# Rotation tables and memory's rstd made without matmuls, in a one-layer decoder kernel

## The chip, the cores and the metric

The kernel runs on one core of one Trainium2 chip. The metric is the device time of one execution in microseconds, as the median of the runs. The engines are named as in the profile: PE is TensorE's matmul side and PEld its weight loads, DVE is VectorE, ACT is ScalarE, POOL is GpSimd, SP is SyncE, which here only issues DMAs. A "q" after a name (SPq) means the engine's sequencer, which issues and waits.

## The reference

One decoder layer on 256 tokens of 1024 features, all in float32. `B` is 1.

```python
h = x + W_out( sig(g_a) * (MoBA(n1 x) W_br_a) + sig(g_b) * (HGRN2(n1 x) W_br_b) )
h = h + CrossAttn(n2 h, n_mem mem)        # 4 heads of 256; mem is 256 tokens
h = h + SwiGLU(n3 h)                      # hidden width 2816
out = rmsnorm(h, final_norm_g)

def rmsnorm(x, g): return x * rsqrt(mean(x * x, -1) + EPS) * g

def rope(t, pos):                          # on q and k of MoBA, 16 heads of 64
    ang = pos[:, None, :, None] * inv_freq # inv_freq = 10000 ** (-arange(0, 64, 2) / 64)
    t1, t2 = t[..., :32], t[..., 32:]
    return concatenate([t1 * cos(ang) - t2 * sin(ang), t2 * cos(ang) + t1 * sin(ang)], -1)
```

Two parts of it matter here: the cosines and sines of `rope` for 256 positions and 32 frequencies, and the rstd of the memory tokens (`rsqrt` of the mean square), which scales the values and the scores of the cross-attention.

## The kernel before

Every weight matrix is read from HBM in chunks of 1 MB (128 partitions x 2048). `prep` loads one chunk (`raw`, L255 to L261), ACT makes its rounded copy `hi` (L266), and DVE makes the rest `lo = raw - hi` (L270). Three matmuls (hi x hi, hi x lo, lo x hi) then give products of full precision. There are three buffers each for `raw`, `hi` and `lo`, and `nxt` prepares chunks two ahead (LEAD = 2). A `raw` buffer comes free when DVE has made `lo`, so SP's next load waits for that.

The order of PE's instructions is the order of the program. The order on ACT, DVE and SP is made by a planner that takes the instruction of the highest rank (the earliest in the program) that it expects to be ready; POOL's order is the program's until L869 or so. Each engine then executes its own list in order, and an instruction that has to wait holds those behind it. On SP this concerns loads: a DMA that waits for data holds the weight loads behind it.

Background work runs in generators. `tick()` is called after each half or whole unit of a matrix product and moves every generator on to its next `yield`. So a `yield` puts what follows one unit (some 5.5 us of PE) later in the program.

The stages in the order of time: the forget gate's matrix with x's norm (to 28 us); the q of HGRN2 (`psf`, to 51); values (`pst`, to 98); q and k of MoBA with rotation (`ev_rope`, to 145); gates and both attentions (to 260); output projections (to 307); the cross-attention, where chunks of q and k alternate with the products P1 to P7 of a Strassen-like scheme for v (to 383); SwiGLU (to 576); the final norm and the stores.

The pieces that the change touches:

- Constants: `cst` (128 x 512 float32) holds the identity for transposes and the causal mask; `lm` (128 x 144) holds HGRN2's masks; `gv` holds gains, the 32 frequencies in each partition and two positions per partition.
- x's rstd: `H` holds the tokens in rows (`xtok`, 1 MB, one transfer, L576). ACT squares both halves with a running sum (L624), `rstd_of` makes `r_x` on POOL (L385), and `rows_of` (L391 to L393) spreads it over partitions by two transposes on PE and a copy on ACT. `spread` places these transposes in the middle of the product for head 5.
- Tables: `rope_tables` reduces the angles on POOL with tokens in partitions, takes both Sin on ACT (L503, L504), and multiplies by `r_x` into `CS` (L507). `angles` (L756) transposes `CS` by four transposes on PE, and ACT copies the result to `turnsF`, with frequencies in partitions and tokens in columns.
- Memory: `mraw` holds memory with features in partitions. `memory()` scales and splits it, squares it in place on ACT (L398), adds pieces on DVE (L401 to L405), and four small matmuls with `ones` sum over partitions (`ssq`, L410). `rows_of` spreads the result by two transposes and a copy. The rows are used in `scores`, the rstd itself in `ev_vx`.
- The last loads: `fetch` (L1431) splits the last loads of SwiGLU into two transfers each.
- The tail: for the second token half, POOL multiplies columns 0 to 512 and 512 to 640 by the final gain, DVE columns 640 to 1024 (L1695); ACT and DVE then scale by the rstd and the stores go out.

Of the kernel before, what the change touches and what calls it, by code (L numbers as in the profile page):

```python
# [12 lines left out]
F32 = mybir.dt.float32  # L13
# [29 lines left out]
C_W = 544  # L43
# [107 lines left out]
def constants():  # L151
# [7 lines left out]
    c[:, C_IF:C_IF + 32] = (10000.0 ** e.astype(np.float64)).astype(np.float32)  # L159
# [14 lines left out]
def build(tc, A, out):  # L174
    nc = tc.nc
    V, SC, G, PE, SY = nc.vector, nc.scalar, nc.gpsimd, nc.tensor, nc.sync
    with ExitStack() as ctx:
# [32 lines left out]
        cst = cp.tile([128, C_IF], F32, name="cst")  # L210
        gv = cp.tile([128, 90], F32, name="gv")
        lm = cp.tile([128, 144], I32, name="lm")
        ifq, posi = gv[:, 56:88], gv[:, 88:90].bitcast(I32)
        nhalf = cp.tile([128, 4], F32, name="nhalf")
        ident = cst[:, C_ID:C_ID + 128]
# [180 lines left out]
        def square(raw, c):  # L396
            a = slice(2 * c, 2 * c + 2)
            SC.activation(raw[:, a], raw[:, a], AF.Square)  # L398
            if c % 2 == 1:
                b = slice(2 * c - 2, 2 * c)  # L400
                V.tensor_tensor(raw[:, a], raw[:, a], raw[:, b], op=ALU.add)  # L401

        def feature_sum(raw):
            V.tensor_tensor(raw[:, 2:4], raw[:, 2:4], raw[:, 6:8], op=ALU.add)
            V.tensor_tensor(raw[:, 2], raw[:, 2], raw[:, 3], op=ALU.add)  # L405

        def feature_rstd(raw, name):
            ps = bank("ssq", (128, 2))
            for t in range(2):
                PE.matmul(ps[:, t:t + 1], raw[:, 2, t * 128:(t + 1) * 128], ones, start=True, stop=True)  # L410
            return rstd_of(ps, name)

# [41 lines left out]
        tables = big("B12", "tables", (128, 1024))  # L454
        CS = tables[:, 0:512].rearrange("p (c i n f) -> p c i n f", c=2, i=2, n=4)
        turnsF = tables[:, 512:1024].rearrange("p (c t) -> p c t", c=2)

        def rope_tables():
            posf = small("posf", [2])
            G.tensor_copy(posf, posi)  # L460
            q = cp.tile([128, 7, 2, 32], F32, name="rt")
# [41 lines left out]
            tc.keep_in_program_order(SC.activation(m, r, AF.Sin))  # L503
            tc.keep_in_program_order(SC.activation(mh, t, AF.Sin))  # L504
# [70 lines left out]
        SY.dma_start(cst, A["cst"])  # L575
        SY.dma_start(H, A["xtok"])  # L576
# [175 lines left out]
        def angles():  # L752
            b = bank("cs", (128, 2, 2, 128))
            for c in range(2):
                for i in range(2):
                    PE.transpose(b[:, c, i], CS[:, c, i].rearrange("p n f -> p (n f)"), ident)  # L756
            SC.activation(turnsF, b.rearrange("p c i t -> p c (i t)"), AF.Copy)

        def hgrn():
# [11 lines left out]
            angles()  # L771
# [169 lines left out]
        def quad(j):  # L941
# [8 lines left out]
            for ss in sc:  # L950
                mx, nm, sums = small("amx", [4]), small("anm", [4]), small("asum", [4])
                two = [t2("ap", (128, 384)) for _ in range(2)]
                for e, (ps, p) in enumerate(zip(ss, two)):
                    for i, (u, w) in enumerate(parts):
                        z = 2 * e + i
                        V.tensor_tensor_reduce(out=p[:, u:w], in0=ps[:, u:w], in1=cst[:, C_MA + u:C_MA + w],
# [125 lines left out]
        def memory():  # L1082
# [15 lines left out]
            mem["rows"] = rows_of(mem["r"], "m", "rowsB")  # L1098
# [680 lines left out]
```

## Time and profile before

| | |
|---|---|
| runs | 588.11, 588.11, 588.49 us, median 588.11 |
| profiled execution, its own time | 588.42 us |
| span of the profiled execution | 586.5 us, 9105 instructions |
| busy in the span | PE 99%, PEld 83%, DVE 78%, ACT 67%, POOL 24% |
| DMA | 155.63 MB, mean 265 GB/s |

The span is the time from the first to the last instruction of the trace; the execution's own time has 1.9 us more around it. Busy time of PE is the union of its matmuls, whose ends are modelled. The trace's views used below are: the busy line, the waits by engine, the chain of waits that ended last (each step followed back to what released it), the timeline of an engine, a tile's instructions, and the DMA issues.

### The profile page before, as it was taken

Reading aid. Unit: us, or ns where it says so; the run is one execution under the profiler, and the core shown is the slowest. Engines: PE = TensorE matmul, PEld = TensorE weight load, DVE = VectorE, ACT = ScalarE, POOL = GpSimd, SP = SyncE. Lnnn points to the kernel's source line nnn. Section 1 sums busy time; section 2 is a strip of 40 time slices with the busy share of each in tenths; the row PEclk is TensorE's granted clock in tenths of the full one; section 3 lists DMA queues with packets and bytes.
Section 4 is the critical chain, followed back from the end, with each engine's and each line's share of the span. In section 5 each row is a group of like instructions: output and inputs, shape, how many; then the busy total and the mean of one; then the engine's idle time right before and its main releaser. Section 6 shows DMA issues by size and latency. Waiting matters only on the chain.

```text
span 586.5 us, 9105 instructions
## 1 busy us (share of the span) xinstructions
PE 579.4 (99%) x3491; PEld 488.5 (83%) x3491; DVE 459.0 (78%) x650; ACT 392.2 (67%) x646; POOL 139.3 (24%) x141
## 2 busy tenths in 40 slices
PE   9999999999999999999999999999999999999995
PEld 7888888888888888888888889988888888888884
DVE  6789968899868774858868786887878788787944
ACT  6796565564686576657459576777858586776744
POOL 4589500466203600003202333200001010100004
PEclk9999999999999999999999999999999999999998
DMA  8865997496993899599866895976879979995801
GB/s 333 339 217 225 326 382 278 153 312 264 268 378 99 225 308 281 202 379 254 253 242 192 277 374 216 244 268 256 353 294 268 391 175 385 259 392 170 310 1 72
DMA packets 22778, 155.63 MB, mean 265 GB/s; under 512 B 2816, under 2 KB 3840, under 8 KB 6528
## 3 DMA queue, kind: packets, MB, share of 16 engines
q1 hardware_dynamic: 18416, 129.12, 56.1%
q0 software_dynamic: 3456, 25.17, 21.9%
q10 hardware_dynamic: 864, 0.77, 0.4%
q8 instruction: 27, 0.44, 0.3%
q14 instruction: 15, 0.12, 0.1%
HBM read 154.00 MB, written 28.31 MB: 311 GB/s over the span
## 4 chain that ended last, share of the span: by engine, by line
PE 94%; DMA 3%; POOL 1%; SPq 0%; ACT 0%; DVE 0%; issue 0%; POOLq 0%; DVEq 0%; ACTq 0%
PE psf L348 13%; PE pqA L1176 11%; PE pst L323 10%; PE pst L325 10%; PE pst L324 10%; PE psf L350 7%; PE pqF L1176 6%; PE acc L323 3%; PE acc L324 3%; PE acc L325 3%; PE pqB L1176 3%; DMA H<-xtok 2%; PE pso L325 1%; PE pso L324 1%; PE pso L323 1%; PE as L946 1%
## 5 line engine op out<-in xcount | busy, mean ns | idle before, releaser
L270 DVE TENSOR_TENSOR lo<-raw,hi 128x1024 fp32r<-128x1024 f32 (+1 forms) x126 | 159.1, 1283 | 33.8 <-ACT hi L266 33.4
L266 ACT ACTIVATE hi<-raw 128x1024 fp32r<-128x1024 f32 (+1 forms) x126 | 125.9, 1028 | 36.1 <-PE pst L325 20.0
L323 PE MATMUL pst<-hi,XX 128*128 128x512 f32 x160 | 63.6, 397 | 0.0
L325 PE MATMUL pst<-hi,XX 128*128 128x512 f32 x160 | 62.4, 390 | 0.0
L324 PE MATMUL pst<-lo,XX 128*128 128x512 f32 x160 | 62.3, 390 | 0.0
L1422 DVE TENSOR_TENSOR lo<-raw,hi 128x2048 fp32r<-128x2048 f32 (+1 forms) x21 | 41.6, 1983 | 11.4 <-ACT hi L1414 11.4
L348 PE MATMUL psf<-XX,hi 128*128 128x512 f32 x192 | 46.7, 392 | 0.0
L1414 ACT ACTIVATE hi<-raw 128x1024 fp32r<-128x1024 f32 x36 | 36.3, 1052 | 13.9 <-PE acc L325 10.3
L348 PEld LDWEIGHTS psf<-XX,hi 128*128 128x128 f32 x192 | 35.1, 188 | 6.8
L323 PEld LDWEIGHTS pst<-hi,XX 128*128 128x128 f32 x160 | 30.0, 188 | 6.9 <-issue 0.7
L325 PEld LDWEIGHTS pst<-hi,XX 128*128 128x128 f32 x160 | 30.0, 188 | 6.4
L336 ACT ACTIVATE ku<-psf 128x256 f32<-128x256 f32 x40 | 15.1, 380 | 30.3 <-PE psf L348 21.5
L324 PEld LDWEIGHTS pst<-lo,XX 128*128 128x128 f32 x160 | 30.1, 188 | 5.9
L1422 DVE TENSOR_TENSOR lo<-b,hi 128x2048 fp32r<-128x2048 f32 x12 | 27.5, 2288 | 9.3 <-ACT hi L1414 9.2
L1414 ACT ACTIVATE hi<-b 128x1024 fp32r<-128x1024 f32 x24 | 24.2, 1053 | 10.4 <-DMA b<-w 5.5
L323 PE MATMUL acc<-hi,hids 128*128 128x512 f32 x70 | 27.4, 392 | 0.0
L325 PE MATMUL acc<-hi,hids 128*128 128x512 f32 x70 | 27.3, 389 | 0.0
L324 PE MATMUL acc<-lo,hids 128*128 128x512 f32 x70 | 27.2, 389 | 0.0
L350 PEld LDWEIGHTS psf<-XX,lo 128*128 128x128 f32 x192 | 24.6, 191 | 0.9
L350 PE MATMUL psf<-XX,lo 128*128 128x256 f32 x192 | 24.9, 283 | 0.0
L1176 PE MATMUL pqA<-hi,SS 128*128 128x512 f32 x72 | 23.9, 393 | 0.0
L1462 POOL DMA_DIRECT2D b<-w x3 | 2.6, 882 | 82.5 <-DVE fu L1528 51.0
(457 smaller groups left out, 1464.7 us busy)
## 6 DMA issues: line engine op xcount, KB each, us to landing
raw<-w SPq DMA_DIRECT2D x72, 1024.0 KB, 6.6
t<-w POOLq DMA_DIRECT2D x13, 1024.0 KB, 12.2
b<-w SPq DMA_DIRECT2D x10, 1024.0 KB, 8.0
raw<-t SPq DMA_DIRECT2D x10, 1024.0 KB, 9.0
b<-w POOLq DMA_DIRECT2D x7, 1024.0 KB, 8.2
raw<-w SPq DMA_DIRECT2D x10, 512.0 KB, 6.9
rawx<-w SPq DMA_DIRECT2D x4, 1024.0 KB, 8.8
b<-t POOLq DMA_DIRECT2D x4, 1024.0 KB, 12.6
```

The lines of the kernel that those rows point to most:

```text
L266: SC.activation(hi[:, a], raw[:, a], AF.Copy)
L270: V.tensor_tensor(lo[:, a], raw[:, a], hi[:, a].bitcast(F32), op=ALU.subtract)
L323: PE.matmul(ps, xh, h, start=first, stop=False)
L324: PE.matmul(ps, xh, l, start=False, stop=False)
L325: PE.matmul(ps, xl, h, start=False, stop=last)
L336: SC.activation(u, ps[:, 1], AF.Copy)
L348: PE.matmul(ps, w[0][:, k, a], X2[:, k], start=begin, stop=end, skip_group_check=m == 1)
L350: PE.matmul(ps[:, 0], w[1][:, k, a], X2[:, k, 0], start=begin, stop=end, skip_group_check=m == 1)
L946: PE.matmul(ps[:, o], qT[r, j, w, q], kT[r, j, w, 0:q.stop], start=w == 0, stop=w == 1)
L1176: PE.matmul(ps, x[k], z[:, k], start=first and k == 0 and i == 0, stop=k == 3 and i == 2, skip_group_check=not first)
L1414: pin(SC.activation(hi[:, a], raw[:, a], AF.Copy))
L1422: pin(V.tensor_tensor(lo[:, a], raw[:, a], hi[:, a].bitcast(F32), op=ALU.subtract))
```

## The change

- The identity becomes a tile of its own (`ident`, 64 KB); the causal mask moves to `lm`, which grows from 72 to 264 KB and is loaded after `H`, as before.
- `H` is loaded in two transfers, one for each half of the tokens.
- The sixth chunk behind the first is prepared in the loop of `last_half`, at m = 2, instead of by the next `nxt`.
- The tables' angles are made with frequencies in partitions (four groups of 32) and 64 positions in columns. After the Sin, SP writes both waves to a DRAM tile, reads them back spread over partitions into `turnsF`, and POOL multiplies by x's rstd in rows. `angles` goes.
- Memory is loaded a second time with tokens in rows (`mtok`, 1 MB, into the buffer of `mraw`). ACT squares it with a running sum; `rstd_of` makes the rstd. SP writes it to a DRAM tile and reads it back as a row in all partitions, behind P2's load. Squares, additions, `ssq` and memory's `rows_of` go.
- Seven instead of five of the last units of SwiGLU are loaded in two transfers each.
- In the tail DVE multiplies columns 512 to 1024 by the gain, and POOL's piece of 128 columns goes.

```diff
-        cst = cp.tile([128, C_IF], F32, name="cst")
-        lm = cp.tile([128, 144], I32, name="lm")
+        ident = cp.tile([128, 128], F32, name="ident")
+        lm = cp.tile([128, 528], I32, name="lm")
+        tri = lm[:, 144:528].bitcast(F32)
...
+        turnsF = big("B12", "turnsF", (128, 2, 256))
+        waves = dr.tile([32, 2, 256], F32, name="waves")
...
-            for i in range(2):
-                G.tensor_scalar(ang[:, i], ifq, posf[:, i:i + 1], None, op0=ALU.mult)
+            G.tensor_copy(ang, posi)
+            G.tensor_scalar(ang, ang, ifq, None, op0=ALU.mult)
...
-            for i in range(2):
-                for c, z in enumerate((mh, m)):
-                    G.tensor_scalar(CS[:, c, i], bc(z[:, i], 4, 1), r_x[:, i:i + 1], None, op0=ALU.mult)
+            yield 1
+            SY.dma_start(waves.rearrange("f c (g t) -> g f c t", g=4), q[:, 1:3])
+            yield 1
+            yield 1
+            SY.dma_start(turnsF, waves.rearrange("(o f) c t -> o f c t", o=1).to_broadcast([4, 32, 2, 256]))
+            yield 1
+            yield 1
+            for c in range(2):
+                G.tensor_tensor(turnsF[:, c], turnsF[:, c], rows_x, op=ALU.mult)
...
-        SY.dma_start(cst, A["cst"])
-        SY.dma_start(H, A["xtok"])
+        SY.dma_start(ident, A["ident"])
+        for t in range(2):
+            SY.dma_start(H[:, t], A["xtok"][:, t])
...
             last_half(1, m, w, spread if m == 1 else None)
+            if m == 2:
+                run(prep())
...
-            angles()
...
-                if k % 2 == 1:
-                    square(raw, k // 2)
...
-            feature_sum(raw)
             yield 1
-            mem["r"] = feature_rstd(raw, "m")
+            mtok = big("B11", "mtok", (128, 2, 1024))
+            SY.dma_start(mtok, A["mtok"])
             yield 1
+            ssqm = small("ssqm", [2])
+            for t in range(2):
+                SC.activation(mtok[:, t], mtok[:, t], AF.Square, accum_out=ssqm[:, t:t + 1])
+            mem["r"] = rstd_of(ssqm, "m")
             yield 1
-            mem["rows"] = rows_of(mem["r"], "m", "rowsB")
+            mem["neg"] = cp.tile([128, 2], F32, name="r_neg")
+            V.tensor_scalar(mem["neg"], mem["r"], -1.0, None, op0=ALU.mult)
+            rd = dr.tile([2, 128], F32, name="rd")
+            SY.dma_start(rd.rearrange("t p -> p t"), mem["r"])
+            for _ in range(6):
+                yield 1
+            mem["rows"] = cp.tile([128, 256], F32, name="rows_m", tag="rowsB")
+            with tc.issue_after(loaded["P2"]):
+                SY.dma_start(mem["rows"], rd.rearrange("(o t) p -> o (t p)", o=1).to_broadcast([128, 256]))
...
-            n = 2 if made_u[0] > len(units) - 5 else 1
+            n = 2 if made_u[0] > len(units) - 7 else 1
...
-            gain(G, hg1[:, 512:640], 1, 512, 640)
-            gain(V, hg1[:, 640:1024], 1, 640, 1024)
+            gain(V, hg1[:, 512:1024], 1, 512, 1024)
```

## Rows read from the trace of the kernel before

**Rows 1.** The page's busy line: busy us (share of the span) x instructions.

```profile
PE 579.4 (99%) x3491; PEld 488.5 (83%) x3491; DVE 459.0 (78%) x650; ACT 392.2 (67%) x646; POOL 139.3 (24%) x141
```

**Rows 2.** Waits of PE: line, waited for, total us, times, longest us.

```profile
PE warm L423 <- PEq L1770: 0.8, 1, 0.8
PE rb L391 <- POOL r_x L385: 0.2, 1, 0.2
PE psg L598 <- ACT hi L266: 0.2, 1, 0.2
```

**Rows 3.** Chain of waits, 0 to 80 us: start us, us, what.

```profile
8.84 12.29 DMA H<-xtok
...
21.21 2.20 ACT junk L624 x4
...
24.47 0.43 PE rb L391 x2
...
26.75 0.95 PE psg L589 x8
```

**Rows 4.** Timeline of PE: start us, us, engine, line, operation, out<-in, forms, count.

```profile
23.12 1.11 PE L589 MATMUL psg<-XX,lo 128*128 128x256 f32 x8
...
81.25 0.66 PE L756 MATMUL cs<-cst,tables 128*128 128x128 f32 x4
81.66 0.48 PE L323 MATMUL pst<-hi,XX 128*128 128x512 f32 x1
...
313.19 0.38 PE L391 MATMUL rb<-cst,r_m 128*128 128x128 f32 x2
313.40 1.04 PE L1136 MATMUL h1T<-cst,H 128*128 128x128 f32 x8
```

**Rows 5.** Chain of waits, whole span.

```profile
301.03 0.34 PE ssq L410 x4
```

**Rows 6.** Timeline of SP, first 20 us.

```profile
8.84 0.45 SPq L576 DMA_DIRECT2D H<-xtok  x1
```

**Rows 7.** The page's DMA issues: out<-in, count, KB each, median us to landing.

```profile
raw<-w SPq DMA_DIRECT2D x72, 1024.0 KB, 6.6
...
raw<-w SPq DMA_DIRECT2D x10, 512.0 KB, 6.9
```

**Rows 8.** Timelines of ACT, SP and DVE, 56 to 76 us.

```profile
56.37 0.24 ACT L504 ACTIVATE rt<-rt 128x64 f32<-128x64 f32 x1
...
60.89 6.99 SPq L257 DMA_DIRECT2D raw<-w  x3
...
72.85 2.01 ACT L266 ACTIVATE hi<-raw 128x1024 fp32r<-128x1024 f32 x2 [1.68 <-DMA raw<-w]
...
73.94 2.36 DVE L270 TENSOR_TENSOR lo<-raw,hi 128x1024 fp32r<-128x1024 f32 x2 [1.27 <-ACT hi L266]
```

**Rows 9.** Tiles mraw and r_m: count, ns min/median/max, first and last start.

```profile
L1087 ACT ACTIVATE mg<-mraw,gv x8: 495/498/500, 261.8 to 270.0; 128x256 f32<-128x256 f32 x8
...
L1222 ACT ACTIVATE vxh<-fc,r_m x2: 724/726/728, 326.1 to 347.7; 128x512 fp32r<-128x512 f32 x2
```

**Rows 10.** DMA issues from 56 to 84 us, columns as in the page's.

```profile
raw<-w SPq DMA_DIRECT2D x6, 1024.0 KB, 10.0
t<-w POOLq DMA_DIRECT2D x2, 1024.0 KB, 13.9
```

**Rows 11.** Timelines of POOL and DVE in the tail.

```profile
580.34 1.99 POOL L1695 TENSOR_TENSOR hg<-H,gf 128x512 f32<-128x512 f32 x2
...
581.19 0.83 DVE L1695 TENSOR_TENSOR hg<-H,gf 128x384 f32<-128x384 f32 x1
...
582.37 0.68 DVE L1733 TENSOR_SCALAR H<-hg,r_f 128x256 f32<-128x256 f32 x2 [0.22 <-POOL hg L1695]
```

**Rows 12.** Timelines of DVE and PE around P4.

```profile
338.91 2.36 DVE L270 TENSOR_TENSOR lo<-b,hi 128x1024 fp32r<-128x1024 f32 x2 [1.43 <-ACT hi L266]
...
341.87 0.39 PE L1176 MATMUL pqF<-hi,M 128*128 128x512 f32 x1
```

More of the change, by code (lines that the diff above doesn't have):

```diff
@@ L42 @@
 C_ID, C_MA, C_IF = 0, 128, 512
-C_W = 544
+C_W = 513
 V_MIX, V_X, V_MEM, V_FFN, V_HG, V_L0, V_L1 = (8 * i for i in range(7))
@@ L158, in constants @@
     e = -np.arange(0, HD, 2, dtype=np.float32) / np.float32(HD)
-    c[:, C_IF:C_IF + 32] = (10000.0 ** e.astype(np.float64)).astype(np.float32)
+    c[:, C_IF] = np.tile((10000.0 ** e.astype(np.float64)).astype(np.float32), 4)
     m = np.zeros((128, 7, 16), np.int32)
@@ L208, in bank @@
             return sm.tile(list(shape), F32, name=name, tag="sm")
[L210 to L213 removed]
+        ident = cp.tile([128, 128], F32, name="ident")
+        gv = cp.tile([128, 121], F32, name="gv")
+        lm = cp.tile([128, 528], I32, name="lm")
+        tri = lm[:, 144:528].bitcast(F32)
+        ifq, posi = gv[:, 56:57], gv[:, 57:121].bitcast(I32)
         nhalf = cp.tile([128, 4], F32, name="nhalf")
[L215 removed]
         H = big("B0", "H", (128, 2, 1024))
@@ L394, in rows_of @@
             return o
[L396 to L411, printed above, removed]
         XX = big("P2", "XX", (128, 8, 2, 256), F32R)
@@ L451, in build @@
             part_x(k)
-        tables = big("B12", "tables", (128, 1024))
-        CS = tables[:, 0:512].rearrange("p (c i n f) -> p c i n f", c=2, i=2, n=4)
-        turnsF = tables[:, 512:1024].rearrange("p (c t) -> p c t", c=2)
+        turnsF = big("B12", "turnsF", (128, 2, 256))
+        waves = dr.tile([32, 2, 256], F32, name="waves")
         def rope_tables():
-            posf = small("posf", [2])
-            G.tensor_copy(posf, posi)
-            q = cp.tile([128, 7, 2, 32], F32, name="rt")
+            q = cp.tile([128, 7, 64], F32, name="rt")
             ang, m, mh, ml, r, t, u = (q[:, i] for i in range(7))
-            for i in range(2):
-                G.tensor_scalar(ang[:, i], ifq, posf[:, i:i + 1], None, op0=ALU.mult)
+            G.tensor_copy(ang, posi)
+            G.tensor_scalar(ang, ang, ifq, None, op0=ALU.mult)
             def rnd(o, src, c):
@@ L502, in rope_tables @@
                 yield 1
-            tc.keep_in_program_order(SC.activation(m, r, AF.Sin))
-            tc.keep_in_program_order(SC.activation(mh, t, AF.Sin))
-            for i in range(2):
-                for c, z in enumerate((mh, m)):
-                    G.tensor_scalar(CS[:, c, i], bc(z[:, i], 4, 1), r_x[:, i:i + 1], None, op0=ALU.mult)
+            tc.keep_in_program_order(SC.activation(mh, r, AF.Sin))
+            tc.keep_in_program_order(SC.activation(m, t, AF.Sin))
+            yield 1
[7 more added lines that the diff above has]
+                G.tensor_tensor(turnsF[:, c], turnsF[:, c], rows_x, op=ALU.mult)
         rt = rope_tables()
@@ L750, in level @@
                     SC.activation(AT[:, 16 + 4 * g:20 + 4 * g], ps, AF.Copy)
[L752 to L757, printed above, removed]
         def hgrn():
@@ L955, in quad @@
                         z = 2 * e + i
-                        V.tensor_tensor_reduce(out=p[:, u:w], in0=ps[:, u:w], in1=cst[:, C_MA + u:C_MA + w],
+                        V.tensor_tensor_reduce(out=p[:, u:w], in0=ps[:, u:w], in1=tri[:, u:w],
                                                op0=ALU.add, op1=ALU.max, scale=1.0, scalar=-3e38,
@@ L1755 @@
     lg = a["hgrn_lb_logits"]
-    positions = np.ascontiguousarray(a["positions"][0].reshape(2, 128).T).astype(np.int32, copy=False)
+    positions = np.repeat(a["positions"][0].astype(np.int32, copy=False).reshape(4, 64), 32, axis=0)
     arrays = {
@@ L1762 @@
         "mT": feats(a["mem"]),
+        "mtok": tokens(a["mem"]),
         "gv": np.ascontiguousarray(np.concatenate(
@@ L1766 @@
         "gfin": np.ascontiguousarray(a["final_norm_g"].reshape(1, D)),
-        "cst": np.ascontiguousarray(cst[:, :C_IF]),
-        "lm": lm,
+        "ident": np.ascontiguousarray(cst[:, :C_MA]),
+        "lm": np.ascontiguousarray(np.concatenate([lm, cst[:, C_MA:C_IF].view(np.int32)], axis=1)),
     }
```

2 lines of the change are left out of this document (removed).

## Prediction

> **What bounds the kernel now.** I read the page's busy line first: PE is busy for 579.4 us of a span of 586.5, 99% [rows 1]. DVE (78%) and ACT (67%) are loaded but not full, so the question for each edit is only whether it takes time off PE's own sequence, or makes PE wait. The view of PE's waits says where it waits at all: three times, 0.8 us at the very start, 0.2 us for the first converted weights, and 0.2 us at L391, where the transposes that spread x's rstd wait for POOL's `r_x` [rows 2]. Everything between the first 25 us and the end is PE doing matmuls back to back, so matmuls that go are worth their full place in the sequence.
>
> The chain of waits then shows what stands behind the L391 stop: tokens in rows `H<-xtok` are asked for at 8.84 and land 12.29 later, ACT squares both halves from 21.21 for 2.20, POOL makes `r_x`, and the transposes start at 24.47 [rows 3]. The group of eight short matmuls before them began at 23.12 [rows 4], and the next such group takes 0.95 in the chain [rows 3]. PE was therefore free at 23.12 + 0.95 = 24.07, and the hole is 24.47 - 24.07 = 0.40 us. The waits view counts half of it because it lets the pipelined tail of the last matmul count as work.
>
> **The change part by part.**
>
> *Matmuls that go.* The four transposes of the tables (`cs`) begin at 81.25 and the next matmul at 81.66: 0.41 us [rows 4]. The four `ssq` matmuls that sum memory's squares hold the chain for 0.34 us [rows 5]. Memory's two `rb` transposes begin at 313.19 and the next group at 313.40: 0.21 us [rows 4]. PE has no idle time around any of them, so the sum is 0.41 + 0.34 + 0.21 = 0.96 us, all on the path.
>
> *Tokens in rows in two transfers, with a smaller constant ahead of them.* 192 KB (the masks) move from ahead of `H` to behind it, and `H` becomes two transfers of 512 KB. The last square then covers one half, 2.20 / 2 = 1.10 us, instead of two. Counted back from before, the start of the second square stood 24.47 - 21.21 - 1.10 = 2.16 us ahead of the transposes. If the second half lands no later than the whole did (8.84 + 12.29 = 21.13), the transposes are ready at about 21.2 + 2.16 = 23.4, 0.7 us before PE wants them at 24.07. So the hole closes even if the second half lands 0.7 us late. One more issue on SP costs about 0.45 [rows 6] against 192 KB less ahead of it, so I take the whole 0.40 us. The bounds are 0 (the order on ACT eats it) and 0.40 (PE can't start before it is free). The load behind it, the fifth chunk's, is asked for one issue later, into a queue that is busy for longer than that anyway.
> On the size of transfers a row and a page differ. The page of the profile has 512 KB loads landing after 6.9 us and 1024 KB loads after 6.6 [rows 7], so halves are not slower as such. The Trainium skill, "DMA: Bandwidth & Descriptors", section "Rules for kernel authors", asks for at least 1 MiB in one DMA for full bandwidth, which speaks against cutting `H`. By the row the hole closes with 0.7 us to spare; by the page the second half could land later and the sum would be 0.40 us smaller.
>
> *Sixth chunk asked for sooner.* Its load is only ranked ahead of the head-pair work, not made possible sooner, since its buffers come free when earlier chunks are used. It reorders ACT and DVE within the first 60 us; I cost it at 0.
>
> *Tables by transposed angles.* POOL works on 128x64 as before. Its four products with r_x go, and two of twice the size come later. ACT loses a copy. What is added: after the Sin at 56.37 [rows 8], SP writes the waves to memory (pieces of 256 B), waits for them to land, and reads them back. Read and product must be done before the first rotation, some 45 us later, which hides them. What isn't plainly hidden is SP: while it waits to issue the read, the weight loads queued behind it wait too. That is a rival below; in the sum it is 0.
>
> *Memory's rstd from rows.* A load of 1 MB (`mtok`) starts when the last scaling of `mraw` is done, at about 270 [rows 9], and lands by about 280 even at the 10.0 us that loads took in the fullest stretch [rows 10]. Two squares, `r`, and the write of 256 numbers follow. The first user of `r` runs at 326.1 [rows 9], so there are some 40 us of cover. ACT trades four squares for two double ones; DVE loses four additions; both are cheaper or equal. The write of 4-byte pieces has no like in the trace: between 0 and the 13.9 us of the slowest transfers shown [rows 10] it stays covered, so 0. The read of the rows is put on SP behind P2's load, which keeps that load out of its wait.
>
> *The tail.* DVE's last scaling starts at 582.37 because POOL's two gains run from 580.34 for 1.99, to 582.33 [rows 11]. POOL's second gain goes; DVE's becomes 512 columns instead of 384. The 384 took 0.83 from 581.19, with POOL beside them, and the reciprocal follows it. Scaled by columns the 512 take 1.1 and end 0.28 later, which would cancel the gain; but POOL stops early now, so part of that is faster. Bounds 0 and 0.18 (582.37 back to 582.19, if the reciprocal doesn't move); I take 0.10. Two more of the last loads in halves cost two issues on an idle SP: 0.
>
> *Sum.* 0.96 + 0.40 + 0.10 = 1.46 us, bounds 0.96 and 1.54. The profiled execution took 588.42 (span 586.5 and 1.9 around it), which would become 586.96. It is 0.31 above the median of the runs, 588.11, and inside their spread. From the median: 588.11 - 1.46 = **586.65**.
>
> **The rivals.**
>
> *Given back to ACT or DVE (about 587.6).* PE comes sooner to every later stage, by up to 1.36 us at 341.87 (0.40 + 0.96). There P4's first matmul starts; the first half of its low part is ready at 338.91 + 2.36 / 2 = 340.09, which is 1.78 us ahead [rows 12]. If the splits don't move along, 0.4 us are left; one more operation of 1.2 us put ahead of such a split makes PE wait 0.8. For it: the planner orders ACT and DVE anew after such edits. Against it: the splits there are released by PE's own progress, mostly, and move with it, and both engines have less to do. Price 0.5 to 1.4: 587.1 to 588.1.
>
> *The hole stays (587.05).* The new order of loads doesn't bring `r_x` sooner: 588.11 - 0.96 - 0.10. Then the change doesn't do what it says in this part.
>
> *SP stands still on the waves (slower, about 590.8).* The read can be issued only when the write has landed, and SP issues in order. The next three loads were issued from 60.89 on, into a stretch in which DMA is so full that ACT waits until the first of them lands, at 72.85 [rows 8]. The first half of its low part takes half of 2.36 from 73.94, so it is ready at 75.1 [rows 8]. PE wants it at 81.66 [rows 4], in the new kernel 0.40 + 0.41 sooner, at 80.85: 5.7 us to spare. So the wait costs nothing until SP is held past 60.89 + 5.7 = 66.6, and makes the kernel slower by over 0.2% past 66.6 + 1.46 + 1.18 = 69.2. If the waves' write, issued at about 56.9, takes as long as POOL's transfers in this stretch, 13.9 us [rows 10], SP is held to 70.8, PE waits 4.2, and the time is 588.11 - 1.46 + 4.2 = 590.8. Against it: SP's own loads in this stretch took 10.0 at the median [rows 10], which ends at 66.9, about where it starts to cost.
> The Trainium skill, the same page, section "Two DMAs through the same engine are not ordered", has the issuing engine wait for the first transfer's semaphore; so SP's stop is the rule, not a mishap, and only its length is open. No run here shows it yet.
>
> **How the numbers follow.** Forecast, everything hidden: 54%, its own range 586.3 to 587.0. Given back: 21%. Hole stays: 10%. SP held: 15%. A measurement of this kernel can tell about 0.2% (1.2 us) from no change, so faster means below 586.93. The forecast is faster by 0.25%, close to that bound: of its 54% I count 52 as faster, with 3 from the near ends of the two middle cases. The rest of those, 30%, is no change; slower is 15%. The range that leaves out the SP case and little else is 586.1 to 588.4.
>
> **What would show it.** Right: no `cs`, `ssq` or memory `rb` on PE, and the L391 wait gone from PE's waits; `h1T` starts some 1.2 us sooner; the last scaling on DVE waits for no POOL. Wrong: a new line in PE's waits. If it is released by a split of chunks 12 to 14 (75 to 95 us), SP's queue was held; if it lies between 28 and 62 or 313 and 345, the order on ACT and DVE gave the gain back. If `H`'s second half lands after 21.8, the hole stays.

## The result: slower by 0.9%, and the profile after

The changed kernel took 594.05 us (median; 591.08 to 596.3), the kernel before 588.11 beside it: a ratio of 1.0092, 95% interval 1.0071 to 1.0113. The forecast was 586.65. The profiled execution of the changed kernel is the longest of its runs, 596.3 us with a span of 594.5; in the shortest the mean granted clock was 0.999, in this one 0.991, and that difference is part of the story.

Busy line of the page of after, columns as in [rows 1]:

```profile
PE 582.0 (98%) x3481; PEld 488.4 (82%) x3481; DVE 457.6 (77%) x646; ACT 391.2 (66%) x644; POOL 130.7 (22%) x137
```

Every engine but PE has less to do than in [rows 1], and ten matmuls are gone. PE is busy for longer all the same, because some of its matmuls ran slowly. So the time did not come from work. Waits of PE in after, columns as in [rows 2]:

```profile
PE pst L323 <- ACT mm L376: 3.6, 1, 3.6
PE pst L323 <- DVE qu L337: 1.6, 1, 1.6
PE warm L406 <- PEq L1759: 0.8, 1, 0.8
PE psg L585 <- ACT hi L266: 0.3, 1, 0.3
PE psf L348 <- DVE qu L337: 0.2, 1, 0.2
PE pst L325 <- DVE mm L376: 0.2, 1, 0.2
```

The wait for `r_x` at L391 of [rows 2] is gone, as forecast. Two large waits stand in its place. The timeline of PE says where, columns as in [rows 4]:

```profile
23.88 0.38 PE L391 MATMUL rb<-ident,r_x 128*128 128x128 f32 x2
...
52.39 0.47 PE L323 MATMUL pst<-hi,XX 128*128 128x512 f32 x1 [1.63 <-DVE qu L337]
...
83.13 0.50 PE L323 MATMUL pst<-hi,XX 128*128 128x512 f32 x1
...
297.95 0.79 PE L323 MATMUL pst<-hi,mm 128*128 128x512 f32 x1 [3.60 <-ACT mm L376]
```

Laid matmul by matmul beside the kernel before, PE's lead or lag runs as follows (each number is the start in after less the start of the same matmul in before, from the two traces):

| place, us in before | after less before | what changed there |
|---|---|---|
| 24.47, `rb` of x | -0.59 | the hole of [rows 3] is closed: -0.40, from -0.19 at the matmul before |
| 45.85 | -0.15 | 0.44 given back |
| 50.74, `pst` | +1.65 | first wait: 1.80 |
| 52.78 | +1.78 | 0.13 more |
| 81.66, behind the tables | +1.47 | `cs` gone: -0.41, from +1.88 at the matmul before |
| 292.71, `pst` | +5.24 | second wait: 3.77 |
| 295.66 | +8.52 | matmuls at the lower clock: 3.28, of it 0.2 a wait for DVE's `mm` |
| 301.23, `h1T` | +8.17 | `ssq` gone: -0.36, from +8.53 |
| 313.40, `h1T` | +7.92 | memory's `rb` gone: -0.21, from +8.13 |

The line at 295.66 needs the stretches of the profile. Each row has the stretch and its length in us, the busy time of PE, PEld, DVE, ACT and POOL, then the granted clock, the DMA share and GB/s; before first:

```profile
290.00:297.00 7.00, 7.00 (x33) 5.79 (x32) 4.47 (x6) 4.26 (x7) 0.00 (x0) 1.00 0.97 282
297.00:305.00 8.00, 8.00 (x43) 6.82 (x42) 4.99 (x8) 4.88 (x9) 0.71 (x1) 1.00 0.64 249
```

and after:

```profile
290.00:297.00 7.00, 4.36 (x22) 3.28 (x20) 1.64 (x2) 0.64 (x1) 0.78 (x1) 1.00 0.62 98
297.00:305.00 8.00, 6.89 (x17) 4.99 (x18) 4.25 (x5) 3.52 (x6) 0.00 (x0) 0.57 0.98 292
```

The traffic fell from 282 to 98 GB/s, PE stood, and then it ran at a granted clock of 0.57 over eight us, that is mostly at 1.2 instead of 2.4 GHz: from 300.35 to 303.76 the matmuls of `pst` begin 0.43 us apart, in before 0.23. The stop costs nearly twice what the waits view shows.

What PE waits for at 297.95 is a split on ACT, and ACT itself was held by a load (timeline of ACT in after):

```profile
296.36 1.06 ACT L266 ACTIVATE hi<-raw 128x1024 fp32r<-128x1024 f32 x1 [7.29 <-DMA raw<-w]
297.32 0.58 ACT L376 ACTIVATE mm<-mT 128x512 fp32r<-128x512 f32 x1
```

The split `mm` had its data; it stands second in ACT's order, behind a weight split whose load came late. The view of the DMA from 268 to 312 us in after: the GB/s in 40 slices of 1.1 us, then issues with KB and median us from issue to landing.

```profile
GB/s 253 104 112 216 216 223 253 350 439 439 395 350 194 268 290 261 305 343 373 171 45 45 0 67 134 238 194 253 276 283 283 283 380 425 406 175 7 104 387 439
...
raw<-w SPq DMA_DIRECT2D x6, 1024.0 KB, 12.6
t<-w POOLq DMA_DIRECT2D x2, 1024.0 KB, 17.5
...
rd<-r_m SPq DMA_DIRECT2D x1, 1.0 KB, 14.3
```

From about 288.9 to 294.4 us five slices in a row hold 171, 45, 45, 0 and 67 GB/s (slices 20 to 24). The write of memory's rstd, `rd<-r_m`, is 1 KB in 256 pieces of 4 bytes. It was issued at 282.11, and its packets ran at 287 to 289 us. The slices behind it are the empty ones.

### The profile page after: what moved, and what is told of

It reads as the page before. It is cut to its first block, busy times and chain, and to the rows that moved or that the text cites. A ratio compares the mean times of both kernels' runs of the same rounds, so it can differ in the third digit from the quotient of the medians.

```text
span 594.5 us, 9083 instructions
## 1 busy us (share of the span) xinstructions
PE 582.0 (98%) x3481; PEld 488.4 (82%) x3481; DVE 457.6 (77%) x646; ACT 391.2 (66%) x644; POOL 130.7 (22%) x137
## 4 chain that ended last, share of the span: by engine, by line
PE 85%; DVE 5%; DMA 4%; ACT 4%; issue 1%; POOL 0%; DVEq 0%; SPq 0%; ACTq 0%; POOLq 0%
PE pqA L1167 11%; PE psf L348 10%; PE pst L323 8%; PE pst L325 8%; PE pst L324 8%; PE pqF L1167 5%; PE psf L350 5%; DMA raw<-w 4%; PE acc L325 3%; PE acc L323 3%; PE acc L324 3%; PE pqB L1167 3%; DVE lo L270 3%; ACT hi L266 1%; PE pso L323 1%; PE pso L325 1%
```

## The experiments

**What is in every one of them.** Unless it says otherwise a kernel is the changed kernel in which TensorE spreads memory's rstd again (`rows_of`, as in before), without the write and the read of the rows; `mtok` and its squares stay. That is e1. Some add a dead write of memory's rstd, which nothing reads. In e7 and all those with a higher number, e11 and e13 apart, GpSimd is held as told under e7. The ratio is to the kernel before on the same chip, the time a median.

| kernel | us | ratio to before, 95% |
|---|---|---|
| changed kernel | 594.05 | 1.0092, 1.0071 to 1.0113 |
| e1_pe_rows | 590.78 | 1.0027, 1.0012 to 1.0043 |
| e5_write_alone (256 x 4 B, side by side) | 594.65 | 1.0091, 1.0061 to 1.0121 |
| e6_write_spaced (256 x 4 B, 512 B apart) | 589.82 | 1.0030, 1.0018 to 1.0042 |
| e11_write_64 (256 x 4 B, 64 B apart) | 591.74 | 1.0055, 1.0039 to 1.0070 |
| e13_write_8 (128 x 8 B, side by side) | 591.13 | 1.0043, 1.0030 to 1.0057 |
| e2_h_one | 589.98 | 1.0018, 1.0004 to 1.0032 |
| e3_pool_held | 589.98 | 1.0029, 1.0009 to 1.0048 |
| e7_pool_waits | 587.88 | 0.9997, 0.9987 to 1.0006 |
| e8_no_sixth | 589.22 | 1.0009, 0.9996 to 1.0022 |
| e9_hold_h_one | 588.46 | 1.0006, 0.9993 to 1.0018 |
| e12_after_held | 593.33 | 1.0083, 1.0068 to 1.0098 |
| e10_mtok_later | 589.08 | 1.0006, 0.9996 to 1.0015 |
| e7b_pool_waits | 587.76 | 0.9994, 0.9986 to 1.0003 |
| e14_squares_held | 587.91 | 0.9992, 0.9984 to 1.0001 |
| e15_held_write_8 | 587.67 | 0.9988, 0.9979 to 0.9997 |
| e16_held_write_64 | 587.74 | 0.9994, 0.9985 to 1.0002 |
| e17_rows_8 | 588.80 | 0.9986, 0.9970 to 1.0001 |
| e18_rows_8_held | 588.01 | 0.9988, 0.9973 to 1.0003 |

### The stop at 298 us: the write, and what about it

e1 takes the write and the read of the rows away:

```diff
-            rd = dr.tile([2, 128], F32, name="rd")
-            SY.dma_start(rd.rearrange("t p -> p t"), mem["r"])
...
+            mem["rows"] = rows_of(mem["r"], "m", "rowsB")
```

> The changed kernel, but memory's rstd is spread to rows by two transposes on PE and a copy, as before; its write in 4-byte pieces and the read of the rows go, the second load of memory (1 MB) and its squares stay. Theory A (the 256 pieces of 4 bytes hold the DMA engines near 289 us, a weight chunk lands some 10 us late, PE stops 3.6 us and runs at the lower clock after it): the stop near 298 us goes, the loads issued at 279 to 291 us land within 10 us again, 589.1 us (588.1, plus 1.47 us that PE is late from 82 to 292 us, less 0.34 for the sums and 0.1 in the tail). Rival B (the extra megabyte crowds the weight loads): the stop stays, 592 to 594 us.

Measured: 1.0027, and no wait near 298 us in the trace. So the write, the read, or SP's stand before the read is the cause. e5 puts the write alone back, with nobody to read it:

```diff
+            rd = dr.tile([2, 128], F32, name="rd")
+            SY.dma_start(rd.rearrange("t p -> p t"), mem["r"])
             mem["rows"] = rows_of(mem["r"], "m", "rowsB")
```

> As e1 (rows by transposes on PE), but memory's rstd is also written to DRAM in 256 pieces of 4 bytes where the changed kernel writes it, and nothing reads it. Theory A: the write alone brings the stop near 298 us back, 592 to 594 us, with packets of several us right behind the small ones. Rival B, or a rival by which SP's wait for the read of the rows costs the time: 589.1 us as e1.

Measured: 1.0091, the whole loss. The write does it, not the read and not a wait of SP. The profiled execution of e5 was its shortest, with a smaller stop; its DMA view has the gap all the same:

```profile
GB/s 380 15 134 149 194 238 231 335 410 425 432 387 238 194 290 290 305 298 396 343 89 104 45 89 134 45 149 186 238 261 246 305 313 439 447 395 454 335 30 156
...
rd<-r_m SPq DMA_DIRECT2D x1, 1.0 KB, 13.8
```

e6 writes the same 256 pieces to places 512 bytes apart:

```diff
+            rd = dr.tile([2, 128, 128], F32, name="rd")
+            SY.dma_start(rd[:, :, 0].rearrange("t p -> p t"), mem["r"])
```

> e1_pe_rows with the write of memory's rstd in 4-byte pieces to DRAM beside it, nobody reading it, but with each piece 512 bytes from the next instead of next to it. Theory A1 (the pieces hold the DMA engines because 256 of them fall into the same 1 KB of DRAM): the loads behind them no longer stand, no PE stop near 298 us, 590 to 591.5 as e1_pe_rows. Theory A2 (a write of 4 bytes costs this wherever it lands): as e5_write_alone, 592 to 596, with the traffic near 290 to 294 us under 100 GB/s and a PE wait for hi there.

Measured: 1.0030, as e1, and the slices behind the write stay filled:

```profile
GB/s 320 97 223 179 194 223 380 454 402 447 328 134 209 223 276 298 305 395 410 439 201 171 194 253 305 246 350 425 417 372 15 119 365 462 22 0 74 335 432 112
...
rd<-r_m SPq DMA_DIRECT2D x1, 1.0 KB, 8.1
```

So 256 pieces of 4 bytes do no harm as such; they do where they lie side by side. e11 (64 bytes apart: the middle size 128 above becomes 16) and e13 (`rd` as `[128, 2]`, written as it lies, 128 pieces of 8 bytes) ask how near is too near.

> e1_pe_rows with the dead write again, its 4-byte pieces 64 bytes from each other (16 KB of DRAM in all). e5_write_alone (4 bytes apart) lost 4 us, e6_write_spaced (512 bytes apart) nothing. If pieces only collide within 64 bytes: no loss, 589.8 to 591. If the unit in which they collide is larger (512 bytes): a loss of its own, 591.5 to 595, with the traffic near 290 us under 100 GB/s.

> e1_pe_rows with the dead write as 128 pieces of 8 bytes, side by side in the same 1 KB, instead of 256 of 4. If the number of pieces sets the loss: half of what e5_write_alone lost, 591.5 to 592.5. If it is that they lie in the same 1 KB, or a step by partition: 593 to 595. If there is no loss, only pieces of 4 bytes do this: 589.8 to 591.

Measured: 1.0055 and 1.0043, in time 591.74, which the expectation had as a loss, and 591.13, between its cases. That settled nothing: neither trace has a stop of over 0.3 us behind the write, but both have another one of 1.1 us ahead of it, near 287 us (below), and they ran on another chip than e1 and e6. So both were run once more on one chip, with the first wait mended (e7, below), beside e7 itself.

> e7_pool_waits with a dead write of memory's rstd as 128 pieces of 8 bytes side by side in 1 KB. e12_after_held, with 256 pieces of 4 bytes there, was at 1.0083 of the kernel before. If nearness within the 1 KB sets the loss whatever the size: as e12, 592.5 to 594. If the number of pieces sets it: about half, 589.8 to 591, with the traffic near 290 us between 45 and 230 GB/s. If 8 bytes are harmless: within 0.4 us of e7b_pool_waits.

> e7_pool_waits with a dead write of memory's rstd as 256 pieces of 4 bytes, 64 bytes from each other. If pieces hold each other up only where they are closer than 64 bytes: within 0.4 us of e7b_pool_waits, as e6_write_spaced was of e1_pe_rows at 512 bytes. If the unit is larger: 590 to 594, with the traffic near 290 us under 100 GB/s.

Measured: 0.9988 and 0.9994 beside 0.9994 for e7b. Pieces 64 bytes apart are harmless, and on this chip so were pieces of 8 bytes. What the write does to the loads can be read packet by packet. This table is from the packets that started between 276 and 304 us; the small ones took 9 or 10 ns in the mean in every kernel with a write, so they are not slow themselves:

| kernel | the write | longest packet of a load, us | packets of loads above 1.5 us | what they took beyond 0.5 us each, summed, us |
|---|---|---|---|---|
| before | none | 1.41 | 0 | 51 |
| e1_pe_rows | none | 1.82 | 4 | 54 |
| e7b_pool_waits | none | 2.22 | 1 | 46 |
| changed kernel | 256 x 4 B, side by side | 6.43 | 27 | 126 |
| e5_write_alone | 256 x 4 B, side by side | 6.14 | 32 | 127 |
| e12_after_held | 256 x 4 B, side by side | 7.07 | 48 | 153 |
| e13_write_8 | 128 x 8 B, side by side | 2.80 | 23 | 82 |
| e17_rows_8 | 128 x 8 B, side by side | 2.21 | 13 | 76 |
| e15_held_write_8 | 128 x 8 B, side by side | 1.97 | 15 | 61 |
| e18_rows_8_held | 128 x 8 B, side by side, at 300 us | 0.90 | 0 | 34 |
| e11_write_64 | 256 x 4 B, 64 B apart | 1.11 | 0 | 49 |
| e16_held_write_64 | 256 x 4 B, 64 B apart | 1.32 | 0 | 53 |
| e6_write_spaced | 256 x 4 B, 512 B apart | 1.45 | 0 | 54 |

Packed pieces of 4 bytes make packets of loads wait 6 to 7 us. Beside packed pieces of 8 bytes, half as many, 13 to 23 packets took 1.5 to 2.8 us in three of four kernels (e18, which writes later, has one of 1.8 up to 312 us); single packets of 2.2 us are there without a write too, so it is their number that tells. Pieces at 64 bytes or more look as if there were no write. That the distance between the pieces decides is shown by e5 beside e6 and e11, which as kernels differ from it in nothing else; what makes near pieces slow is not. The Trainium skill, "DMA: Bandwidth & Descriptors", section "Rules for kernel authors", says that a strided last dimension lowers to one descriptor for each element and is to be rearranged. The trace agrees on the 256 pieces; but e16 has as many and loses nothing, so by these runs their number alone is not the price.

### The wait at 52 us: GpSimd beside VectorE

PE waits there for a PSUM bank, whose eviction on DVE (L337) comes 3.0 us late. Timelines of DVE and POOL in before:

```profile
46.91 0.83 DVE L566 TENSOR_TENSOR QK<-QQ,fT 128x256 f32<-128x256 f32 x2
...
48.80 0.74 DVE L337 TENSOR_TENSOR qu<-psf,ku 128x256 f32<-128x256 f32 x2
...
50.07 1.94 POOL L690 TENSOR_TENSOR Tt<-fT 128x1024 f32<-128x1024 f32 x1
...
57.74 8.51 POOL L507 TENSOR_SCALAR tables<-rt,r_x 128x128 f32<-128x128 f32 x4
```

and in after:

```profile
47.07 3.29 DVE L552 TENSOR_TENSOR QK<-QQ,fT 128x256 f32<-128x256 f32 x2
50.28 1.63 DVE L270 TENSOR_TENSOR lo<-raw,hi 128x1024 fp32r<-128x1024 f32 x1
51.83 0.74 DVE L337 TENSOR_TENSOR qu<-psf,ku 128x256 f32<-128x256 f32 x2
...
46.16 2.73 POOL L679 TENSOR_TENSOR Tt<-fT 128x1024 f32<-128x1024 f32 x1
48.98 4.03 POOL L679 TENSOR_TENSOR Tt<-Tt 128x512 f32<-128x512 f32 x5
```

DVE's order in this stretch is the same. But POOL reaches its first level product 3.9 us sooner: 1.6 because `r_x` is (22.05 instead of 23.68), and 2.3 because the 32 operations on `rt` between the two, as many as before, took 19.5 instead of 21.8 us in all. Why they were quicker is not shown. The four products with `r_x` that go have no part in it, as they stood behind the level products (57.74). The product now lies beside the two QK products, which take 3.29 instead of 0.83. One by one: POOL's product ends at 48.90 and the first QK at 49.18; POOL's second product ends at 50.08 and the second QK at 50.36. Each time DVE ends 0.28 us behind POOL.

e3 tried to hold POOL by ranking its product behind the eviction. The rank did not hold POOL, so the product began at 46.68, beside QK (47.59, 3.29 us) as in e1, and the kernel tells nothing on this.

> As e1, and POOL's first product for HGRN2's levels is issued only after DVE's eviction of the third q unit. Theory C: that eviction is back at about 48.8 us as before, PE's wait at 52 us is gone, 589.1 - 2.2 = 586.9 us. Rival D: the eviction and the wait stay, 589.1 us.

Measured: 1.0029, as e1. e7 holds it at run time, by an operand:

```diff
                 V.tensor_tensor(u, u, rows_x, op=ALU.mult)
+                if (c, m) == (2, 1):
+                    seen[0] = G.tensor_copy(cp.tile([128, 1], F32, name="seen"), u[:, 0:1]).ins
...
+                    with tc.issue_after(seen[0]) if L == 1 else nullcontext():
                         G.tensor_tensor(tview(2 * L), T0, Tq, op=ALU.mult)
```

> Memory's rstd is spread by TensorE as in e1_pe_rows, and GpSimd copies one column of the evicted query unit (the one whose bank the matmuls wait for) ahead of its first level product, so that the product can't start before that eviction. Theory C (the wait at 52 us comes from GpSimd's product of 128x1024 lying beside VectorE's two QK products): the two QK products take 0.8 us again instead of 3.3, the 1.7 us wait of pst for the eviction of line 337 is gone, and the kernel is 1.6 to 2 us faster than e1_pe_rows, 588.7 to 589.3 beside 588.85 for the kernel before. Rival (QK is slow for a reason of its own, or VectorE is late for another one): QK keeps 3.3 us, the wait stays, 590.6 to 591. Second rival: the wait goes, but the level products come later and the level matmuls wait for them, a new PE wait of about 1 us at 66 to 75 us: 589.8 to 590.5.

Measured: 0.9997, 0.3% or 1.8 us below e1's ratio. Timelines of DVE and POOL in e7:

```profile
47.47 0.75 DVE L556 TENSOR_TENSOR QK<-QQ,fT 128x256 f32<-128x256 f32 x2
...
50.76 2.92 POOL L552 COPY seen<-qu 128x1 f32<-128x1 f32 x1 [4.15 <-DVE qu L550]
53.65 1.89 POOL L684 TENSOR_TENSOR Tt<-fT 128x1024 f32<-128x1024 f32 x1
```

QK is back at 0.75, and the wait is gone from PE's waits. The copy of one column fits this from the other side: on POOL it took 2.92 us, beside DVE's splits, and ended at 53.68, 0.04 behind one of them. The Trainium skill, "SBUF — State Buffer", section "SBUF: two separate sides", says that GpSimd and a VectorE instruction with two SBUF inputs share a port pair that one of them holds for a whole instruction while the other stands. The trace agrees: 0.41 us of QK became 2.11, up to the end of POOL's product.

Whether the two losses add was asked by putting the hold into the changed kernel as it is, write and all.

> The changed kernel as it is, its write of 4-byte pieces too, with GpSimd's first level product held as in e7_pool_waits. Theory (the two losses are independent and add): the wait near 52 us goes, the stop near 290 to 298 stays, so about 1.8 us faster than the changed kernel, 591.5 to 593. Rival (with TensorE 1.8 us earlier the loads stand behind the write for longer on its path, as it has less lead to lose): the stop grows by what the first gave, 593.5 to 594.5.

Measured: 1.0083 beside 1.0092, with overlapping intervals. The trace has the wait at 52 us gone, a stop of 1.1 at 287, and 3.4 us of waits of `pst` at 292 to 299 with the clock at 0.79 behind them. Matmul by matmul, PE is 1.65 us ahead of the changed kernel at 81.66 and 0.44 behind it at 286.31, as the stop at 287 takes 1.26 here and nothing there; the stop behind the write then takes 2.05 less, and at the end e12 is 1.69 ahead. That is one execution of each. Within the intervals of the times it stays open whether the losses add.

### Two smaller parts

e2 and e9 ask for the tokens in rows in one transfer, on e1 and on e7:

> As e1, and tokens in rows in one transfer again. Theory C (x's rstd comes sooner, so POOL reaches its first product for HGRN2's levels at 46.2 instead of 50.1 us and slows DVE's products and evictions just when PE waits for a bank at 52.4): POOL's product starts about 1 us later than in e1, PE's wait at 52 us falls from 1.8 to under 1 us, about 588 us. Rival D (the order that the sixth chunk's rank gives DVE and ACT makes the eviction late): the wait stays at 1.8 us, 589.1 to 589.5 us.

> e7_pool_waits with the tokens in rows in one transfer, as in the kernel before. Theory (the two halves only bring r_x forward by 0.5 to 1 us, which TensorE does not need as the spread of it comes some us later): within 0.3 us of e7_pool_waits. Rival (the halves are needed to close the hole at the spread of r_x): a PE wait for rb of about 0.4 us and 0.4 us slower.

Measured: 1.0018 against 1.0027, and 1.0006 against 0.9997. Both differences are inside the intervals and of opposite sign: two transfers or one, nothing that can be measured. In e2 the wait at 52 us stays at 1.6 and POOL's first level product begins at 46.51, so the two halves are not what brings that product forward. e8 leaves out the earlier request for the sixth chunk:

> e7_pool_waits without the earlier request for the sixth weight chunk. Theory (the sixth chunk's request has no part in either loss): within 0.3 us of e7_pool_waits. Rival (the earlier request is what lets VectorE and ScalarE run the chunks' splits ahead, or what delays the tokens in rows): more than 0.5 us away from it, with a PE wait for hi or lo near 45 us if it is needed, or an earlier r_x if it did harm.

Measured: 1.0009 against 0.9997. The intervals overlap, but the trace has a PE wait much as the rival named it, for an eviction instead of a split (waits of e8):

```profile
PE psf L348 <- DVE qu L337: 0.9, 1, 0.9
```

It lies at 40.3 us; e7 has one by this name of 0.3, at 45.3. By PE's lag at 45.85 (0.82 in e8, 0.25 in e7) the earlier request is worth about 0.6 us in this new order; by the times alone it can't be told.

### A third stop, near 287 us

In some executions the transposes of `tat` wait 0.9 to 1.1 us for POOL. Waits of PE in e7, and then its timelines of ACT and DVE:

```profile
PE mT L1040 <- POOL tat L1035: 1.0, 1, 1.0
```

```profile
278.48 1.06 ACT L1083 ACTIVATE mtok<-mtok 128x1024 f32<-128x1024 f32 x1 [4.63 <-DMA mtok<-mtok]
...
280.71 0.17 DVE L383 TENSOR_SCALAR v__3196<-ssqm 128x2 f32<-128x2 f32 x1 [3.19 <-ACT mtok L1083]
```

ACT stands 4.6 us for memory's second load, DVE 3.2 behind it, and `tat` comes late. Set the start of the squares, less PE's lag behind the kernel before at 81.66 us, beside this stop: in the ten kernels without it the squares start at 274.8 to 277.7 on that scale (the changed kernel: 278.89 - 1.47 = 277.4); in the seven with it (e2, e7, e8, e10 to e13) at 278.4 to 280.2. No kernel lies in between. So the stop goes with a late landing of `mtok` against PE, and how late it lands changes from one execution and chip to another.

e10 asked for the squares two steps later; ScalarE's order came out the same, ACT stood 6.15 us, and so it tested nothing.

> e7_pool_waits with memory's squares two steps further behind the load of mtok, and nothing else moved. In e7_pool_waits ScalarE stands 4.6 us at 278 for mtok to land, VectorE 3.2 us behind it, and TensorE then 1.0 us at 287 for the transposes of tat. Theory (the third stop is mtok's landing): ScalarE's wait for mtok falls under 1 us, the wait of mT for tat is gone, 0.7 to 1 us faster than e7_pool_waits, 586.9 to 587.2 beside 588.4 for the kernel before. Rival (GpSimd's product or VectorE's splits set the end of tat): the wait of 1.0 us stays, within 0.3 us of e7_pool_waits.

Measured: 1.0006. e14 moves them in the order itself:

```diff
+            with tc.issue_after(seen["turn"]):
                 for t in range(2):
                     SC.activation(mtok[:, t], mtok[:, t], AF.Square, accum_out=ssqm[:, t:t + 1])
```

> e7_pool_waits with memory's squares queued on ScalarE behind the last split of the merged tokens' transposes (near 293 us instead of 278); the order on TensorE and SyncE is the same. Theory (the stop of 1.0 us of the transposes of tat near 287 us comes from ScalarE standing for mtok's load, and VectorE behind it): no wait of ScalarE for mtok, the wait of mT for tat is gone, 0.7 to 1.2 us faster than e7b_pool_waits beside it. Rival (what is moved only stops something else: the squares now stand ahead of the hidden state's squares and of the split of a weight chunk near 295 us): a new PE wait of 0.5 to 2 us at 295 to 305 us, within 0.4 us of e7b_pool_waits or slower. Second rival (the weights behind it in the queue are late, not ScalarE): the wait of mT stays.

> e7_pool_waits once more, beside the others of this call, since chips differ in how soon the load of mtok lands. 587.5 to 589.2: as e7_pool_waits if the stop near 287 us is there in some runs only, as e10_mtok_later if it is there in most.

Measured: 0.9992 and 0.9994. e14 has no such stop and no wait for `mtok`, but on this chip e7b had none either (its squares started at 277.87 with a lag of 0.22). Moving the squares costs nothing; that it cures the stop is not shown.

### The change as it was meant

e17 is the changed kernel with the hold of e7, and with its write and read in pieces of 8 bytes:

```diff
-            rd = dr.tile([2, 128], F32, name="rd")
-            SY.dma_start(rd.rearrange("t p -> p t"), mem["r"])
+            rd = dr.tile([128, 2], F32, name="rd")
+            SY.dma_start(rd, mem["r"])
...
-                SY.dma_start(mem["rows"], rd.rearrange("(o t) p -> o (t p)", o=1).to_broadcast([128, 256]))
+                SY.dma_start(mem["rows"], rd.rearrange("(o p) t -> o (p t)", o=1).to_broadcast([128, 256]))
```

> The changed kernel with its two losses mended and nothing else: GpSimd's first level product held behind the query unit's eviction, and memory's rstd written to DRAM as 128 pieces of 8 bytes (token pairs as they lie) and read back in that order; the eight scaled maxima of line 1288 read the rows through a view with a step of two. Theory (the change's gains stand once the losses are gone): no wait near 52 us, none near 298, none for rb at 313; 0.2 us faster than e15_held_write_8, so 0.5 to 1 us faster than the kernel before, ratio 0.998 to 0.999. Rival (the read of the rows, behind loads at 300 us, or the maxima with a step of two, cost what the spread cost): as e15 or slower, ratio 0.999 to 1.0005. Rival (the stop near 287 us, if mtok lands late on this chip): 1 us more.

> e17_rows_8 with memory's squares behind the last split of the merged tokens, as in e14_squares_held; the write then goes out near 296 us, and the read of the rows right behind it on SyncE's queue. Theory (the stop near 287 us comes from ScalarE's wait for mtok): where e17_rows_8 shows that stop, it is gone and the kernel 0.7 to 1.2 us faster; where e17 shows none, within 0.3 us of it. Rival (SyncE stands at the read until the write has landed, 7 to 9 us as such writes took, and the weights' requests behind it come late): a PE wait for hi or lo of 0.5 to 2 us at 310 to 325 us, slower than e17 by as much.

Measured: 0.9986 (0.9970 to 1.0001) and 0.9988 (0.9973 to 1.0003). That is where the theory had them, but both intervals reach 1, and e17's median, 588.80, is no better than the 588.72 of the kernel before beside it. Its profiled execution, the longest of its runs, has a stop (waits of PE, then a stretch):

```profile
PE pst L323 <- ACT mm L376: 2.1, 1, 2.1
```

```profile
290.00:297.00 7.00, 4.67 (x16) 3.02 (x16) 2.67 (x3) 2.49 (x3) 0.00 (x0) 0.85 1.00 188
```

It is where the old stop was, and shorter. Of the four kernels with pieces of 8 bytes this one alone shows it. The 13 slow packets of the table start at 290.5 to 294.4, right behind the write, which speaks for the write as its cause; but loads took 13.6 us at the median here (10.4 in e15), and no kernel like e17 with another write or none was run, so the cause of this stop is not shown. e18, with the squares and so the write later, shows no stop at all, and SP stood at the read from 297.30 to 302.58 without a wait on PE. The only kernel here whose interval lies below 1 is e15, at 0.9988: everything of the change but memory's rows read, GpSimd held, and a write that serves nothing.

## Why the prediction was wrong, step by step

**Matmuls that go: right.** Put at 0.41, 0.34 and 0.21; the table of PE's lag has 0.41, 0.36 and 0.21, in all 0.98 for 0.96.

**The hole at L391: the 0.40 us came, and did not stay.** At `rb` the lag falls by 0.40 in the changed kernel and in every kernel of the experiments. (What stands ahead of `rb`, from 0.19 sooner to 2.02 later in these traces, differs between executions, so the lag at the end of one trace is not the worth of a change.) Between `rb` and 45.85 the changed kernel gives 0.44 back, and e7 0.54: PE comes sooner to a bank whose eviction on DVE comes no sooner. Timelines of DVE in before and in after, then of PE in after:

```profile
44.44 0.75 DVE L337 TENSOR_TENSOR qu<-psf,ku 128x256 f32<-128x256 f32 x2
```

```profile
44.43 0.74 DVE L337 TENSOR_TENSOR qu<-psf,ku 128x256 f32<-128x256 f32 x2
...
44.90 1.43 PE L348 MATMUL psf<-XX,hi 128*128 128x512 f32 x5 [0.20 <-DVE qu L337]
```

The term was worth about nothing. This is the rival "given back to ACT or DVE", in the stretch from 28 to 62 us that the prediction named, a little under its price of 0.5 to 1.4.

**"POOL works on 128x64 as before": the first failed step.** The prediction asked what waits for POOL, not what POOL's work lies beside. With the level product 3.9 us sooner it lay on DVE's QK products, and PE lost 1.80 us at 50.74; e7 against e1 shows it. In the tail the prediction itself counted on DVE being quicker once POOL stops, but it did not ask this here. Its sign for a wait between 28 and 62 us (the order on ACT and DVE) would have named a wrong cause, since DVE's order there is the same. The sixth chunk, costed at 0 for reordering ACT and DVE, is not the step that failed: without it e8 is later, not sooner.

**Tables by way of DRAM: right.** The rival in which SP stands still on the waves did not decide. Timeline of SP in after:

```profile
56.64 0.68 SPq L486 DMA_DIRECT2D waves<-rt  x1
...
63.24 0.59 SPq L489 DMA_DIRECT2D turnsF<-waves  x1
63.93 0.42 SPq L257 DMA_DIRECT2D raw<-w  x1
```

SP could issue the read 6.6 us behind the write, when the waves had landed, and the next load went out at 63.93, ahead of the 66.6 from which a wait costs. PE waits for no split there.

**Memory's rstd: "the write of 4-byte pieces has no like in the trace: between 0 and the 13.9 us [...] it stays covered, so 0": the step that cost most.** Both ends of that bound are times until the write itself lands. It took 14.3, about as the upper end had it, and its own users were covered as forecast (`rows` read at 300.82, used from 366). What it does to the transfers beside it was not asked. In the profiled execution the stop cost 3.77 us as a wait and 3.28 behind it, nearly all of that as clock; e1 and e5 show that the write is the cause. The bound should have held a near stop of the traffic while the write is under way, against the slack of the loads in flight then. For the waves the prediction set a delay of SP against the slack of the loads behind it; here it set nothing against the loads.

**"ACT trades four squares for two double ones": right as work, wrong as a place.** ACT stands for `mtok` in its order. Where `mtok` lands late against PE, a stop of 0.9 to 1.1 us goes with it; the changed kernel's profiled execution, in which PE was 1.5 us late by then, has none.

**The tail: right in kind, smaller.** From DVE's last addition to its last scaling before took 582.37 - 580.60 = 1.77 us ([rows 11] and the first row below, of before); after, 590.43 - 588.69 = 1.74. So 0.03 for 0.10. In the other eighteen traces the end of the span lies between 0.02 us sooner and 0.17 later against PE's last matmul than in before, so no gain of this term was measured.

```profile
580.60 0.42 DVE L1688 TENSOR_TENSOR H<-end,H 128x256 f32<-128x256 f32 x1 [0.29 <-PE end L325]
```

```profile
588.69 0.42 DVE L1677 TENSOR_TENSOR H<-end,H 128x256 f32<-128x256 f32 x1 [0.29 <-PE end L325]
...
590.43 0.68 DVE L1721 TENSOR_SCALAR H<-hg,r_f 128x256 f32<-128x256 f32 x2
```

**The sum.** Gains of 0.98 + 0.03 were there to be kept, where 1.46 were forecast. With both losses out, e15 and e16 ended at a span of 585.9 for 586.5, a gain of 0.6 with memory's `rb` still in, and 0.5 and 0.4 by the medians on the same chip. In e15 that is 0.41 of `cs` and 0.36 of `ssq`, the hole's 0.40 less 0.43 given back, and 0.15 lost ahead of `rb`. So the gain side was right for the matmuls that go and too high by the hole. On the loss side the one rival that made the kernel slower (SP held) did not decide, and the two mechanisms that did had no price.

## What to carry to other kernels

A transfer in tiny pieces is to be priced by what it does to the loads beside it, not only by when it lands: here 256 pieces of 4 bytes did no harm once they lay 64 bytes apart. When an edit brings GpSimd forward, lay its long products beside VectorE's timeline and see which two-input instructions they now meet; if those feed TensorE, hold GpSimd by an operand. A stop of TensorE costs more than it lasts where the granted clock falls behind it, so one stop of 3.6 us cost 7.05, nearly five times the 1.46 forecast for all the edits together.

## What the runs showed of the hardware that was not expected

- 256 writes of 4 bytes into 1 KB of DRAM, 9 ns each as packets, leave the DMA traffic at 0 to 67 GB/s for four slices of 1.1 us (45, 45, 0, 67), and packets of other transfers at up to 6.4 us (7.1 in e12); at 64 bytes apart the same 256 pieces leave no trace (longest packet 1.3 us).
- A QK product of 0.41 us took 2.11 beside a product on GpSimd, and ended 0.28 behind it; a copy of one column on GpSimd took 2.92 beside VectorE's splits.
- After a stop of 3.6 us TensorE's granted clock was 0.57 over the next 8 us, and the matmuls behind it came 3.28 us later on top.
- Kernels with the same order up to there met their load of `mtok` later or sooner by some us from one chip and execution to another (the squares began at 277.84 in e6 and at 281.20 in e11, with PE's lag 1.78 and 1.95), enough to make a stop of 1 us come and go.
